# Hybrid decoder trunk on one core: the second feed-forward product taken one Strassen product at a time, its sum over the chunks kept in PSUM, and local attention's mask added by VectorE in the instruction that takes the maximum

## The chip, the cores and the metric

The kernel runs on one core of a Trainium2 chip. The core has a matrix engine (TensorE, PE in the profile, with its weight loads as PEld), three engines for elementwise work (VectorE or DVE, ScalarE or ACT, GpSimd or POOL) and a queue that issues transfers (SyncE, SP). They run side by side and wait for each other through semaphores. The metric is the device time of one execution in microseconds (us).

## The reference, cut to what matters

Two layers, 1024 tokens of width 1024, everything in float32:

```
for l in range(2):
    h = rms_norm(x, mix_norm_g[l])
    proj = h @ w_in[l]              # q, k, v of two attention branches, gates
    o_sb  = stick_breaking_attention(...)          # 8 heads
    o_swa = sliding_window_sink_attention(...)     # 8 heads, 2 key/value heads, window 128
    merged = gates[0] * (o_sb @ w_branch_sb[l]) + gates[1] * (o_swa @ w_branch_swa[l])
    x = x + merged @ w_out[l]
    h2 = rms_norm(x, mlp_norm_g[l])
    x = x + square(relu(h2 @ w_up[l])) @ w_down[l] # widths 1024 -> 4096 -> 1024
```

In local attention a block of 128 queries sees 256 keys (its own block and the one before). Scores outside the window count as minus infinity, and a learned sink per head joins the softmax: its maximum and its sum take the sink in, its output does not.

## The kernel before, in words

Every float32 product is made of three passes: each operand is split into a high part (fp32r, by ACT) and the rest (the original less the high part, by DVE), and PE computes high·high, high·low and low·high into one PSUM bank (`three`, L346 to L349).

The order of the instructions on each engine is written out ahead of time by a small planner in Python. It runs a model of the five engines and of the transfers (`Plan`): each process yields the engine that it needs and a cost, or an event or a slot to wait for, and whichever process is ready first (or has the lower rank) issues its instruction. On the chip each engine then takes its instructions strictly in that order. The costs of the model are plain numbers: `act(n)`, `dve(n)`, `mm(n)`; a transfer costs `moved(n)`, and the `LINK` table has the delay from one engine's end to the next one's start (M is the transfers, so MA is the delay from a landing to ACT).

Stages of a layer: norm of x and its transposes, gates and local attention (SWA) woven together, stick-breaking attention, merge and output projection, norm, first feed-forward product (`up_phase`), second feed-forward product (`down_phase`). There are 8 PSUM banks.

**Local attention** (`iteration` in `swa_phase`): 16 iterations in each layer, one for each of 2 key heads and 8 blocks of 128 queries, at most three in flight. Each has two PSUM banks of scores, two heads in each. Into a bank PE first writes the mask (L694: identity times a bf16 tile of zeros and -1e30, 128x512), then adds the four score matmuls (L698, 128x256 each). DVE takes the maximum of a bank (L702), two small instructions turn it into the exponent's bias (L713, L715), and ACT reads the bank with a scale and that bias, writes the exponential to `pr` in SBUF and sums it (L724).

**Second feed-forward product** (`down_phase`): u = square(relu(...)), of 1024 x 4096, is cut along its 4096 columns into four chunks c. A chunk is a 1024x1024 by 1024x1024 product, done by seven half-size products (Strassen's scheme in Winograd's form) named 1, 2, 5, 3, 6, 7, 4 in that order. The left operands (sums and differences of u's blocks) were formed in the up phase and wait in DRAM (`u_scr`). The right operands are the four quadrants 11, 12, 21, 22 of the chunk of w_down for products 1, 2 and 3, and differences of them for 5, 6, 7 and 4. A product is 4 row tiles i by 4 depth tiles j by 3 passes, 48 matmuls of 128x512. The loops run over chunks outside and products inside, `for c: for n in order`.

Before a product both its operands are split into an `operand` tile each (ACT L1273, DVE L1276, four instructions of 128x1024 on each engine for the two operands). There are five operand tiles: four of the pool "act", one of the pool "op". The differences of w_down's quadrants are made by POOL in place (`sums`, L1290, 128x512), through a tile t for product 5. At the end of every product of every chunk DVE adds the four PSUM banks to x or to an accumulator in SBUF (`collect`, L1287, L1888): 1, 5 and 6 have accumulators, which are added to the quadrants of x in the last chunk.

Between the layers the driver starts the next norm: DVE writes the normed tile `h` (L426), PE transposes it (L437), ACT and DVE split it into hT.

All transfers go through SP's queue, in the order of the plan.

Of the kernel before, what the change touches and what calls it, by code (L numbers as in the profile page):

```python
# [16 lines left out]
P = 128  # L17
# [39 lines left out]
ORDER = ("1", "2", "5", "3", "6", "7", "4")  # L57

# [48 lines left out]
class Plan:  # L107
# [6 lines left out]
    LINK = {"PA": .2, "PD": .2, "AP": .3, "DP": .26, "GP": .3, "PP": 0.0, "GD": .1, "SS": 0.0, "SM": .65, "MA": .9, "MD": .9, "MG": .9, "MP": .9, "MS": .9}  # L114
# [82 lines left out]
def tile_hybrid_trunk(ctx: ExitStack, tc: tile.TileContext, x, g_mix, g_mlp, g_rope, sinks, rope,  # L197
# [40 lines left out]
    win_mask = cp.tile([P, 256], BF16, name="win_mask")  # L238
    first_mask = cp.tile([P, 256], BF16, name="first_mask")
    nc.gpsimd.memset(win_mask, 0.0)  # L240
    nc.gpsimd.memset(first_mask, NEG)
    prev, cur = win_mask[:, 0:P], win_mask[:, P:256]
    nc.gpsimd.affine_select(out=prev, in_=prev, compare_op=ALU.is_gt, fill=NEG, base=0,
                            pattern=[[1, P]], channel_multiplier=-1)
    nc.gpsimd.affine_select(out=cur, in_=cur, compare_op=ALU.is_ge, fill=NEG, base=0,
                            pattern=[[-1, P]], channel_multiplier=1)
    nc.gpsimd.tensor_copy(first_mask[:, P:256], cur)
# [20 lines left out]
    def moved(n):  # L268

        return "M", n / 250e3, 0  # L270
# [210 lines left out]
    def swa_phase(l, base, sw, swp, hT, normed, o_scr, tab_scr, finished, tail, projected):  # L481
# [15 lines left out]
        def consts(g):  # L497
# [11 lines left out]
            if g == 0:  # L509
                yield "G", gps(512)  # L510
                nc.gpsimd.tensor_scalar(gt[:, :, 0:4], gt[:, :, 0:4], 0.125, None, ALU.mult)
# [45 lines left out]
        def iteration(g, t):  # L557
# [123 lines left out]
            msk = (first_mask if t == 0 else win_mask).unsqueeze(1).broadcast_to([P, 2, 256])  # L681
# [5 lines left out]
            zs = {}  # L687

            def scores(i):
                bz = Bank("z")  # L690
                yield from bz.take()
                yield "P", .71
                sc = bz.tile().rearrange("p (a b) -> p a b", a=2)
                nc.tensor.matmul(sc, ident_b, msk, start=True, stop=False)  # L694
                for j in range(2):
                    h = 2 * i + j
                    for kk in range(2):
                        nc.tensor.matmul(sc[:, j, lo_col:256], qst[:, h * P:(h + 1) * P], keys_[:, kk],  # L698
                                         start=False, stop=kk == 1 and j == 1)
# [3 lines left out]
                zs[i] = sc, bz  # L703
# [4 lines left out]
            yield e_y  # L708
            y5 = e_y.value
            yield e_z  # L710

            yield "D", .12
            nc.vector.scalar_tensor_tensor(mx4, mx4, -1.0, y5[:, 0:4], ALU.mult, ALU.mult)  # L713
            yield "D", .12
            nc.vector.tensor_tensor(mx4, mx4, snk[:, 1], ALU.min)  # L715
            e_s = Event(plan, 3)

            def expo(i):
                sc, bz = zs[i]
# [5 lines left out]
                bz.free()  # L725
# [947 lines left out]
    def down_phase(l, base, quads, u_scr, u_ev, tail_raw, tail_ring, wide, acc_on, x_ev, x3_ev, dst, saved, splits_done, finished):  # L1673
        r0 = base + 84000
        order = ORDER

        kinds_ = {("b", "11"): "wh", ("b", "12"): "wl", ("b", "21"): None, ("b", "22"): None}
        turns = [(c, n, j) for c in range(4) for n in order for j in range(2)]
        ring_of = (("raw", None), ("raw", None), ("wl", 0), ("wl", 1), ("wh", 2), ("wh", 3))
        spot = [Slots(plan, 1) for _ in ring_of]  # L1680
        fetched_a = {t: Event(plan) for t in turns}
        place = {(s, q, j): Slots(plan, 1) for s, q in kinds_ for j in range(2)}
        came = {(c, s, q, j): Event(plan) for c in range(4) for s, q in kinds_ for j in range(2)}
# [9 lines left out]
        def load(c, s, q, j):  # L1693
            yield place[s, q, j]
            if kinds_[s, q] is None:
                yield wide
# [27 lines left out]
        def cutting(c, n, j):  # L1724
# [11 lines left out]
            if c == 3:  # L1736
                splits_done.set()
# [433 lines left out]
```

## Time and profile before

| | us |
|---|---|
| median of 3 runs (lowest to highest) | 2814.79 (2811.83 to 2817.49) |
| the profiled execution's own time | 2815.18 |
| its span, from the first to the last instruction | 2813.4 |
| TensorE's mean granted clock, as a share of 2.4 GHz | 0.993 |

Busy time counts an instruction from start to end; matmuls overlap a little, so "busy" of PE also covers the part of an instruction that lies beside the next one. A row of instructions reads: line, engine, operation, output<-inputs, shapes, count | busy us, mean ns of one | idle time of the engine just before them, and what ended it. In a timeline a row begins with the start and the duration in us; idle time before it stands in brackets. A row of a table of stretches has: from:to in us, its length, then busy us (and instructions) of PE, PEld, DVE, ACT and POOL, the granted clock of TensorE (1.00 is 2.4 GHz, 0.50 is 1.2 GHz), the busy share of the transfer engines, and GB/s.

### The profile page before, as it was taken

What the parts mean: (1) busy time and instruction counts of PE and PEld (TensorE: products, weight loads), DVE (VectorE), ACT (ScalarE), POOL (GpSimd) and SP (SyncE); (2) the same over time, 40 slices, a digit from 0 to 9 for tenths busy, and PEclk for the clock granted to TensorE, in tenths of its full rate; (3) what the DMA queues carried; (4) which work ended last, traced back from release to release, by engine and by line L of the source; (5) the groups of instructions that cost most, each with busy time, mean ns of one, the idle gap of its engine ahead of it and who ended that gap; (6) DMA issues with size and microseconds to landing.
All of it is one profiled execution on the core that took longest, in us unless ns stands there. A gap on an engine that the chain in (4) does not pass through costs nothing.

```text
span 2813.4 us, 37269 instructions
## 1 busy us (share of the span) xinstructions
PE 2727.7 (97%) x13632; PEld 2293.8 (82%) x13632; DVE 2035.9 (72%) x3223; ACT 1269.9 (45%) x2561; POOL 493.7 (18%) x387
## 2 busy tenths in 40 slices
PE   6999999999989999999899999999999999999998
PEld 6888888888868887877678888888887788877877
DVE  5565788855587878777865657887646877777788
ACT  4776566552432223433347765655524322244332
POOL 1000000000032334323510000000000332253225
PEclk9999999999999999999999999999999999999999
DMA  4232221164034447444232222222631344564442
GB/s 164 71 91 70 60 61 58 54 228 165 31 105 161 155 143 260 151 156 144 84 116 81 80 66 59 66 56 81 220 142 31 128 146 157 157 250 154 146 151 74
DMA packets 138647, 335.50 MB, mean 119 GB/s; under 512 B 16352, under 2 KB 30688, under 8 KB 138464
## 3 DMA queue, kind: packets, MB, share of 16 engines
q1 hardware_dynamic: 138464, 333.13, 35.6%
q8 instruction: 107, 1.75, 0.3%
q14 instruction: 76, 0.62, 0.1%
HBM read 227.16 MB, written 97.52 MB: 115 GB/s over the span
## 4 chain that ended last, share of the span: by engine, by line
PE 84%; DVE 9%; ACT 4%; issue 2%; DMA 1%; POOL 1%; SPq 0%; DVEq 0%; ACTq 0%; POOLq 0%
PE bank L347 24%; PE bank L348 24%; PE bank L349 24%; DVE operand L1276 3%; PE bank L1057 2%; PE bank L1090 1%; PE bank L986 1%; PE bank L987 1%; PE bank L1089 1%; ACT pr L724 1%; PE bank L437 1%; PE bank L698 1%; DVE xt L1287 1%; PE bank L768 1%; DVE acc L1287 1%
## 5 line engine op out<-in xcount | busy, mean ns | idle before, releaser
L348 PE MATMUL bank<-operand 128*128 128x512 f32 x896 | 353.4, 394 | 27.9 <-DVE operand L1276 27.9
L347 PE MATMUL bank<-operand 128*128 128x512 f32 x896 | 351.7, 393 | 0.0
L349 PE MATMUL bank<-operand 128*128 128x512 f32 x896 | 350.8, 392 | 0.0
L1273 ACT CAST operand<-dr 128x1024 fp32r<-128x1024 f32 x208 | 205.0, 1051 | 291.4 <-PE bank L349 241.6
L1276 DVE TENSOR_TENSOR operand<-dr,operand 128x1024 fp32r<-128x1024 f32 x208 | 289.2, 1425 | 32.9 <-ACT operand L1273 32.7
L347 PE MATMUL bank<-hT,wh 128*128 128x512 f32 (+1 forms) x776 | 311.4, 401 | 1.5 <-ACT hT L394 1.5
L349 PE MATMUL bank<-hT,wl 128*128 128x512 f32 (+1 forms) x776 | 303.1, 391 | 0.0
L348 PE MATMUL bank<-hT,wh 128*128 128x512 f32 (+1 forms) x776 | 302.5, 390 | 0.1
L1273 ACT CAST wh<-raw 128x512 fp32r<-128x512 f32 x128 | 79.4, 620 | 386.2 <-DMA raw<-in_w_up_dram 201.0
L348 PEld LDWEIGHTS bank<-operand 128*128 128x128 f32 x896 | 169.5, 189 | 70.4 <-DVE operand L1276 35.9
L1290 POOL TENSOR_TENSOR stage<-raw 128x512 f32<-128x512 f32 x32 | 58.2, 1820 | 832.7 <-DMA raw<-in_w_up_dram 557.1
L347 PEld LDWEIGHTS bank<-operand 128*128 128x128 f32 x896 | 169.7, 189 | 35.6
L349 PEld LDWEIGHTS bank<-operand 128*128 128x128 f32 x896 | 169.8, 189 | 35.1
L349 PEld LDWEIGHTS bank<-hT,wl 128*128 128x128 f32 x776 | 146.8, 189 | 31.8
L347 PEld LDWEIGHTS bank<-hT,wh 128*128 128x128 f32 x776 | 147.5, 190 | 25.3 <-ACT hT L394 1.9
L348 PEld LDWEIGHTS bank<-hT,wh 128*128 128x128 f32 x776 | 147.4, 190 | 24.4 <-DVE hT L396 0.4
L336 DVE TENSOR_TENSOR wl<-raw,wh 128x1024 fp32r<-128x1024 f32 x88 | 107.5, 1222 | 71.4 <-ACT wh L333 70.8
L1287 DVE TENSOR_TENSOR xt<-xt,bank 128x512 f32<-128x512 f32 x160 | 106.3, 682 | 69.9 <-PE bank L349 69.7
L333 ACT CAST wh<-raw 128x1024 fp32r<-128x1024 f32 x88 | 92.4, 1050 | 111.5 <-PE bank L349 76.6
L1290 POOL TENSOR_TENSOR dr<-dr 128x512 f32<-128x512 f32 x64 | 115.5, 1821 | 38.3 <-issue 38.3
L1006 DVE TENSOR_TENSOR_SCAN keep<-keep 128x128 f32<-128x128 f32 (+3 forms) x128 | 99.8, 809 | 19.1 <-ACT keep L995 18.8
L1065 DVE TENSOR_TENSOR tl<-bank,th 128x512 fp32r<-128x512 f32 (+1 forms) x160 | 97.8, 629 | 20.2 <-ACT th L1063 18.9
(217 smaller groups left out, 7099.7 us busy)
## 6 DMA issues: line engine op xcount, KB each, us to landing
dr<-u_scr SPq DMA_DIRECT2D x112, 512.0 KB, 4.6
u_scr<-up SPq DMA_DIRECT2D x160, 256.0 KB, 2.6
raw<-in_w_up_dram SPq DMA_DIRECT2D x68, 512.0 KB, 4.2
dr<-in_w_down_dram SPq DMA_DIRECT2D x64, 512.0 KB, 4.3
raw<-in_w_gate_dram SPq DMA_DIRECT2D x32, 512.0 KB, 4.0
g_scr<-stage SPq DMA_DIRECT2D x64, 256.0 KB, 2.3
gate<-g_scr SPq DMA_DIRECT2D x64, 256.0 KB, 3.8
u_scr<-stage SPq DMA_DIRECT2D x64, 256.0 KB, 2.4
```

The source lines that it names most:

```text
L333: nc.scalar.copy(hi[:, :n], raw[:, :n])
L336: nc.vector.tensor_tensor(lo[:, :n], raw[:, :n], f32(hi[:, :n]), ALU.subtract)
L347: nc.tensor.matmul(ps_ap, ah, bh, start=first, stop=False)
L348: nc.tensor.matmul(ps_ap, ah, bl, start=False, stop=False)
L349: nc.tensor.matmul(ps_ap, al, bh, start=False, stop=last)
L1006: nc.vector.tensor_tensor_scan(later[:, ::-1], later[:, ::-1], later[:, ::-1], ini, ALU.mult, ALU.bypass)
L1057: nc.tensor.transpose(tr[:, i * P:(i + 1) * P], w[:, j * P - c0:(j + 1) * P - c0], ident)
L1065: nc.vector.tensor_tensor(tl[:, :n], tr[:, :n], f32(th[:, :n]), ALU.subtract)
L1273: nc.scalar.copy(op.hi(j, n), src)
L1276: nc.vector.tensor_tensor(op.lo(j, n), src, f32(op.hi(j, n)), ALU.subtract)
L1287: nc.vector.tensor_tensor(out, a, b, op)
L1290: nc.gpsimd.tensor_tensor(out, a, b, op)
```

## The change

There are three parts. The first two change what is computed where; the third changes two numbers of the planner's model, and with them the order that it writes on every engine.

1. Local attention: the mask matmuls (L694) go. The score matmuls start the bank themselves. For each head DVE runs one `tensor_tensor_reduce`: the scores (now negated, as q is scaled by -0.125) times y, with the float32 mask (+1e30) added, are written to `pr` and their minimum together with the negated sink is taken. It is built as two instructions, the pass over 128x256 and a short one that writes out the minimum. ACT then exponentiates `pr` in place. The two small instructions L713 and L715 and the reduce L702 go.
2. Second feed-forward product: the loops change places, `for n in DOWN: for c in range(4)`, with the products in the order 1, 5, 2, 6, 3, 7, 4. A product adds its four chunks in the same four PSUM banks, and DVE adds the banks to x's quadrants once, after the fourth chunk (56 additions of 128x512 in a layer; no accumulators). The quadrants of w_down are read again for each product that needs them: 88 reads of 512 KB in a layer (16 of them from `t_scr`) where there were 32, and two differences, those of products 5 and 6, are stored to `t_scr` in DRAM (16 stores) to be read back for 6 and 4. The differences are now made by DVE (128x1024), none by POOL. Six operand tiles instead of five; six places for left operands as before, and eleven for right operands.
3. The planner: the delay after a landing is 2.0 instead of 0.9, and transfers move 380e3 instead of 250e3 in its units.

```diff
+DOWN = ("1", "5", "2", "6", "3", "7", "4")
+LATE_RAWS = 3
...
-    LINK = {..., "SM": .65, "MA": .9, "MD": .9, "MG": .9, "MP": .9, "MS": .9}
+    LINK = {..., "SM": .65, "MA": 2.0, "MD": 2.0, "MG": 2.0, "MP": 2.0, "MS": 2.0}
...
-        return "M", n / 250e3, 0
+        return "M", n / 380e3, 0
...
-                yield "P", .71
+                yield "P", .48
                 sc = bz.tile().rearrange("p (a b) -> p a b", a=2)
-                nc.tensor.matmul(sc, ident_b, msk, start=True, stop=False)
                 for j in range(2):
                     h = 2 * i + j
                     for kk in range(2):
                         nc.tensor.matmul(sc[:, j, lo_col:256], qst[:, h * P:(h + 1) * P], keys_[:, kk],
-                                         start=False, stop=kk == 1 and j == 1)
+                                         start=kk == 0, stop=kk == 1)
                 z_use.done()
-                yield "D", dve(512)
-                nc.vector.tensor_reduce(mx4[:, 2 * i:2 * i + 2], sc, AX.X, ALU.max)
+                yield e_y
+                y5 = e_y.value
+                for j in range(2):
+                    h = 2 * i + j
+                    yield "D", dve(256)
+                    nc.vector.tensor_tensor_reduce(pr[:, h, lo_col:], sc[:, j, lo_col:], win_mask[:, lo_col:], y5[:, h:h + 1],
+                                                   snk[:, 1, h:h + 1], ALU.add, ALU.min, mx4[:, h:h + 1])
+                bz.free()
...
-                    nc.scalar.activation(pr[:, h], sc[:, j], AF.Exp, bias=mx4[:, h:h + 1], scale=y5[:, h:h + 1], accum_out=sm4[:, h:h + 1])
+                    nc.scalar.activation(pr[:, h, lo_col:], pr[:, h, lo_col:], AF.Exp, bias=mx4[:, h:h + 1], scale=-1.0, accum_out=sm4[:, h:h + 1])
...
+        order = DOWN
+        steps = [(n, c) for n in order for c in range(4)]
+        turns = [(n, c, j) for n, c in steps for j in range(2)]
+        a_ring = (("raw", None), ("raw", None), ("wl", 0), ("wl", 1), ("wh", 2), ("wh", 3))
+        b_ring = (("wh", 0), ("wh", 1), ("wl", 2), ("wl", 3)) + (("dr", None),) * 4 + (("late", None),) * LATE_RAWS
...
+        parts = {"1": ("11",), "2": ("21",), "5": ("12", "11"), "6": ("22", "t0"), "3": ("22",), "7": ("22", "12"), "4": ("21", "t1")}
+        keeps_ = {"5": 0, "6": 1}
...
+        opx = Slots(plan, 2)
...
+                        if m % 6 < 4:
+                            yield acts
...
+        def stream_b():
+            for n, c, j in turns:
+                for q in parts[n]:
+                    i = yield from pb.take()
+                    if q[0] == "t":
+                        yield t_in[int(q[1]), c, j]
+                        src = t_scr[int(q[1]), c, j]
+                    else:
+                        src = w_down[l, c, "12".index(q[0]) * 2 + "12".index(q[1]), j]
+                    yield "S", .45
+                    raw = pb.tile(i)
+                    nc.sync.dma_start(out=raw, in_=src)
...
+        def cut_b(n, c, j):
+            qs = parts[n]
+            yield b_in[(n, c, j), qs[0]]
+            raw, i = b_in[(n, c, j), qs[0]].value
+            use = Shared(2 if n in keeps_ else 1, lambda: pb.release(i))
+            if len(qs) > 1:
+                yield b_in[(n, c, j), qs[1]]
+                other, i2 = b_in[(n, c, j), qs[1]].value
+                yield from two("D", raw, raw, other, ALU.subtract, 1024)
+                pb.release(i2)
+                if n in keeps_:
+                    plan.spawn(keep(n, c, j, raw, use), plan.cur.rank)
+            yield ops[n, c, "b"]
+            yield from split(ops[n, c, "b"].value, 2 * j, raw, 1024)
...
+        def keep(n, c, j, raw, use):
+            yield "S", .45
+            nc.sync.dma_start(out=t_scr[keeps_[n], c, j], in_=raw)
...
+        sums = {"1": ("11", "12", "21", "22"), "2": ("11",), "5": ("12", "22"), "6": ("12", "21", "22"), "3": ("12",), "7": ("21", "22"), "4": ("21",)}
+        def product(n, c, i):
...
+                three(state[n, i][1], s.hi(j)[:, cs], s.lo(j)[:, cs], t.hi(j), t.lo(j), c == 0 and j == 0, c == 3 and j == 3)
...
+        def collect(n, i):
+            b, pm = state.pop((n, i))
+            for q in sums[n]:
+                t, h = i + 4 * (q[0] == "2"), int(q[1]) - 1
+                yield x_ev[t]
+                yield "D", dve(512)
+                xs = x_ev[t].value[:, h * 512:(h + 1) * 512]
+                nc.vector.tensor_tensor(xs, xs, pm, ALU.add)
```

**What moves on PE in local attention.** PE's order around the scores of an iteration in the first layer, before (wg is the weight of the q, k, v projection, ks and qst the split keys and queries, pr the probabilities):

```order
L349 MATMUL bank<-hT,wl 128x512
L694 LDWEIGHTS ident_b
L694 MATMUL bank<-win_mask,ident_b 128x512
L698 MATMUL bank<-ks,qst 128x256 x4
L694 LDWEIGHTS ident_b
L694 MATMUL bank<-win_mask,ident_b 128x512
L698 MATMUL bank<-ks,qst 128x256 x4
L347 MATMUL bank<-hT,wh 128x512
```

The same place in the changed kernel:

```order
L348 MATMUL bank<-hT,wl 128x512
L694 MATMUL bank<-ks,qst 128x256 x8
L346 MATMUL bank<-hT,wh 128x512
L347 MATMUL bank<-hT,wh 128x512
L348 MATMUL bank<-hT,wl 128x512
L761 MATMUL bank<-ident,pr 128x128 x4
```

The eight score matmuls of an iteration now stand together, without a mask matmul and its weight load; what fills the time until the transposes of pr is gate work (hT, wh), as before.

**What moves on SP in the second feed-forward product.** SP's queue for the loads of one whole chunk in the first layer, before (u_scr holds the left operands, in_w_down_dram the right ones):

```order
L1721 DMA dr<-u_scr_7323 128x1024 x8
L1704 DMA dr<-in_w_down_dram 128x1024
L1721 DMA dr<-u_scr_7323 128x1024 x2
L1704 DMA dr<-in_w_down_dram 128x1024 x3
L1721 DMA dr<-u_scr_7323 128x1024 x2
L1704 DMA dr<-in_w_down_dram 128x1024 x2
L1721 DMA dr<-u_scr_7323 128x1024 x2
L1704 DMA dr<-in_w_down_dram 128x1024 x2
```

SP's queue in the changed kernel, for the last loads of product 1 and the first of product 5 (t_scr takes the stored differences):

```order
L1770 DMA dr<-in_w_down_dram 128x1024 x11
L1818 DMA t_scr_7289<-dr 128x1024
L1756 DMA dr<-u_scr_7288 128x1024 x2
L1818 DMA t_scr_7289<-dr 128x1024
L1770 DMA dr<-in_w_down_dram 128x1024 x2
L1818 DMA t_scr_7289<-dr 128x1024
L1770 DMA dr<-in_w_down_dram 128x1024 x2
L1818 DMA t_scr_7289<-dr 128x1024 x2
L1770 DMA dr<-in_w_down_dram 128x1024 x2
L1756 DMA dr<-u_scr_7288 128x1024 x2
L1770 DMA dr<-in_w_down_dram 128x1024 x4
```

Before, a chunk had 14 loads of u and 8 of w_down. Now stores stand among the loads, and each of them waits for DVE's subtraction before the load behind it can be issued.

**What moves on DVE where the first layer ends.** DVE's order before the first normed tile h of the second layer, before (xt_7304 to xt_7311 are the eight row tiles of x, `v`, `rs_a` and `y` the small instructions of the norm):

```order
L1287 TENSOR_TENSOR xt_7308<-xt_7308,bank 128x512
L422 TENSOR_SCALAR v<-ss 128x1
L1287 TENSOR_TENSOR xt_7309<-xt_7309,bank 128x512 x2
L360 TENSOR_TENSOR rs_a<-y 128x1
L422 TENSOR_SCALAR v<-ss 128x1
L362 TENSOR_TENSOR rs_a<-rs_a,v 128x1
L364 TENSOR_SCALAR rs_a<-rs_a 128x1
L422 TENSOR_SCALAR v<-ss 128x1
L366 TENSOR_TENSOR y<-y,rs_a 128x1
L360 TENSOR_TENSOR rs_a<-y 128x1
L1287 TENSOR_TENSOR xt_7310<-xt_7310,bank 128x512
L426 SCALAR_TENSOR_TENSOR h<-xt_7304,y,g 128x1024
```

The same place in the changed kernel (xt_7269 is the first row tile, xt_7276 the last):

```order
L1863 TENSOR_TENSOR xt_7276<-xt_7276,bank 128x512
L1269 TENSOR_TENSOR operand<-dr,operand 128x1024 x7
L421 TENSOR_SCALAR v<-ss 128x1 x3
L359 TENSOR_TENSOR rs_a<-y 128x1
L361 TENSOR_TENSOR rs_a<-rs_a,v 128x1
L363 TENSOR_SCALAR rs_a<-rs_a 128x1
L365 TENSOR_TENSOR y<-y,rs_a 128x1
L425 SCALAR_TENSOR_TENSOR h<-xt_7269,y,g 128x1024
```

Before, the first h stood behind additions of the last product but one (7, into xt_7308 to xt_7310). Now it stands behind the last splits of operands alone; product 7's additions come earlier, since four chunks of product 4 follow it. On PE the first transposes of h stand 48 matmuls before the end of `down_phase` in the first layer before, and 90 matmuls before it now.

## Rows read from the trace of the kernel before

**Rows 1.** The page, busy time of the engines.
```profile
PE 2727.7 (97%) x13632; PEld 2293.8 (82%) x13632; DVE 2035.9 (72%) x3223; ACT 1269.9 (45%) x2561; POOL 493.7 (18%) x387
```

**Rows 2.** Waits of PE, whole span: total us, times, longest us.
```profile
PE bank L348 <- DVE operand L1276: 27.9, 17, 2.9
```

**Rows 3.** Stretches: the second feed-forward product of both layers.
```profile
1086.90:1401.20 314.30, 300.05 (x1297) 244.59 (x1295) 244.71 (x246) 116.88 (x134) 126.75 (x74) 0.99 0.43 150
2488.00:2809.70 321.70, 307.97 (x1340) 251.62 (x1339) 251.02 (x257) 113.41 (x128) 130.02 (x76) 0.99 0.44 151
```

**Rows 4.** Timeline of PE: one of six such waits.
```profile
1199.10 0.50 PE L348 MATMUL bank<-operand 128*128 128x512 f32 x1 [2.86 <-DVE operand L1276]
```

**Rows 5.** Timelines of ACT, DVE and POOL ahead of that wait.
```profile
1190.62 3.90 ACT L1273 CAST operand<-dr 128x1024 fp32r<-128x1024 f32 x4 [4.20 <-PE bank L349]
...
1191.70 6.75 DVE L1276 TENSOR_TENSOR operand<-dr,operand 128x1024 fp32r<-128x1024 f32 x3 [0.39 <-ACT operand L1273]
1198.97 1.21 DVE L1276 TENSOR_TENSOR operand<-dr,operand 128x1024 fp32r<-128x1024 f32 x1
...
1192.88 4.49 POOL L1290 TENSOR_TENSOR dr<-dr 128x512 f32<-128x512 f32 x2
```

**Rows 6.** Stretches in which TensorE's granted clock was at its lower level.
```profile
1200.30:1203.70 3.40, 3.40 (x9) 2.66 (x9) 1.22 (x1) 0.62 (x1) 3.32 (x3) 0.51 0.69 243
1405.10:1411.90 6.80, 3.91 (x14) 3.43 (x15) 6.34 (x25) 4.45 (x11) 0.00 (x0) 0.50 0.47 180
2599.80:2603.20 3.40, 3.40 (x10) 2.62 (x9) 1.22 (x1) 0.62 (x1) 3.32 (x3) 0.50 0.67 222
```

**Rows 7.** Timeline of PE: two banks of scores, from mask to mask.
```profile
189.34 0.38 PE L694 MATMUL bank<-win_mask,ident_b 128*128 128x512 bf16 x1
...
190.04 0.39 PE L694 MATMUL bank<-win_mask,ident_b 128*128 128x512 bf16 x1
```

**Rows 8.** Stretch: local attention of the first layer, past its start.
```profile
100.00:250.00 150.00, 149.41 (x864) 131.12 (x863) 93.20 (x260) 113.63 (x327) 1.89 (x3) 1.00 0.26 79
```

**Rows 9.** Groups of instructions: local attention's softmax, and their nearest kin.
```profile
L702 DVE TENSOR_REDUCE mx<-bank 128x2 f32<-128x512 f32 x64 | 42.1, 684 | 9.3 <-PE bank L698 9.3
L713 DVE SCALAR_TENSOR_TENSOR mx<-mx,y 128x4 f32<-128x4 f32 x32 | 5.0, 157 | 0.4
...
L1097 DVE TENSOR_TENSOR o<-o,bank 64x256 f32<-64x256 f32 x64 | 26.0, 406 | 16.2 <-ACT o L1095 16.0
L724 ACT ACTIVATION_READ_ACCUMULATOR pr<-bank,mx,y 128x1 f32 x128 | 25.8, 201 | 0.0
L1006 DVE TENSOR_TENSOR_SCAN keep<-keep 128x256 f32<-128x256 f32 x32 | 21.5, 673 | 0.0
```

**Rows 10.** Groups of instructions: splits and additions of the second feed-forward product.
```profile
L1276 DVE TENSOR_TENSOR operand<-dr,operand 128x1024 fp32r<-128x1024 f32 x208 | 289.2, 1425 | 32.9 <-ACT operand L1273 32.7
L1273 ACT CAST operand<-dr 128x1024 fp32r<-128x1024 f32 x208 | 205.0, 1051 | 291.4 <-PE bank L349 241.6 <-DMA dr<-u_scr 23.1 <-DVE acc L1287 17.8
L1287 DVE TENSOR_TENSOR xt<-xt,bank 128x512 f32<-128x512 f32 x160 | 106.3, 682 | 69.9 <-PE bank L349 69.7
```

**Rows 11.** Stretches in which the transfer engines were full.
```profile
1085.00:1095.00 10.00, 9.69 (x44) 7.68 (x43) 9.96 (x11) 6.19 (x8) 1.35 (x1) 1.00 1.03 413
2500.00:2510.00 10.00, 10.00 (x45) 8.25 (x45) 5.77 (x7) 2.63 (x3) 9.92 (x6) 1.00 1.06 343
```

**Rows 12.** Waits of PE from 1086 to 1130 us, then from 2486 to 2530.
```profile
PE bank L348 <- DVE operand L1276: 4.1, 5, 1.7
...
PE bank L348 <- DVE operand L1276: 3.6, 4, 1.6
```

**Rows 13.** Timelines of PE and DVE where the second layer begins.
```profile
1407.99 1.97 PE L437 MATMUL bank<-ident,h 128*128 128x128 f32 x8 [6.88 <-DVE h L426]
...
1406.65 1.28 DVE L426 SCALAR_TENSOR_TENSOR h<-xt,y,g 128x1024 f32<-128x1024 f32 x1
```

**Rows 14.** Transfers issued from 1086 to 1115 us: KB each, us to landing.
```profile
dr<-in_w_down_dram SPq DMA_DIRECT2D x5, 512.0 KB, 9.9
```

More of the change, by code (lines that the diff above doesn't have):

```diff
@@ new lines, in release, with lay @@
+            def release(self, i):
+                p = self.spots[i]
+                if i in self.final:
+                    tag, unit = self.ring[p]
+                    if unit is not None:
+                        give[unit].done()
+                    elif tag == "raw":
+                        raws.release()
+                else:
+                    self.free[p].release()
+            def lay(self, skip, first):
+                n, spots = len(self.ring), []
+                while len(spots) < self.count:
+                    spots += [p for p in range(n) if len(spots) + p >= first or p not in skip]
+                self.spots = spots[:self.count]
+                self.final = {max(i for i, p in enumerate(self.spots) if p == q) for q in set(self.spots)}
@@ L1718, in stream, with arrive, stream_a @@
+        def arrive(ev, raw, i):
+            yield moved(1024 * 512)
+            ev.set((raw, i))
+        def stream_a():
+            for n, c, j in turns:
+                i = yield from pa.take()
                 yield u_ev[c, n]
                 yield "S", .45
-                raw = wp.tile([P, 1024], F32, tag=tag, name="dr", bufs=2 if tag == "raw" else 4)
-                nc.sync.dma_start(out=raw.rearrange("p (a b) -> p a b", a=2), in_=u_scr[7 * c + order.index(n), :, 2 * j:2 * j + 2])
@@ L1739, in arrive @@
-        def arrive(ev, raw):
-            yield moved(1024 * 512)
-            ev.set(raw)
-        def loads(group):
-            for c in range(4):
-                for s, q in group:
-                    for j in range(2):
-                        yield from load(c, s, q, j)
-        def free(c, s, q, j):
-            if c < 3:
-                place[s, q, j].release()
-            elif kinds_[s, q] is not None:
-                give[j + 2 * (q == "12")].done()
-        opx = Slots(plan, 1)
@@ L1758, in operands @@
+        ops = {(n, c, s): Event(plan) for n, c in steps for s in "ab"}
+        opx = Slots(plan, 2)
         def operands():
@@ L1817, in cut_sum @@
-        def cut_sum(s, op, k, t):
-            yield from split(op, k, t, 512)
-            tmp_use[s].pop(0)()
-        tmp_use = {"a": [], "b": []}
-        def frees(c):
-            def one(s, q, j, evs):
-                for e in evs:
-                    yield e
-                free(c, s, q, j)
-                if c == 3:
-                    splits_done.set()
-            for s in "b":
-                for q in ("11", "12", "21", "22"):
-                    n = [m for m in order if m != "5" and (m, s) in source and source[m, s] == q][-1]
-                    for j in range(2):
-                        plan.spawn(one(s, q, j, [cut[c, n, s, j], summed[c, s, j]]), r0)
@@ L1853, in product @@
             yield s.ready[0]
             yield t.ready[0]
[L1855 to L1856 removed]
+            if c == 0:
+                b = Bank("md")
+                yield from b.take()
+                state[n, i] = [b, None]
+            else:
+                yield begun[n, c - 1, i]
             cs = slice(i * P, (i + 1) * P)
```

315 lines of the change are left out of this document (99 added, 216 removed).

## The prediction

> **What bounds the kernel now.** I read the page's busy times first. PE is busy for 2727.7 of 2813.4 us, the next engine for 72% [rows 1]; the reader is to see that nothing but PE's own work and its 86 idle us can give much. Then I asked who ends PE's waits: the largest line by far is DVE's split of an operand of the second feed-forward product, 27.9 us in 17 waits [rows 2]. The table of stretches puts it in place: in the two runs of that product PE is busy for 300.05 of 314.30 us and for 307.97 of 321.70 us, so 14.2 and 13.7 us are idle [rows 3]. The timelines show why. In each layer three waits are of some 2.9 us like the one at 1199.10 [rows 4]. Ahead of it ACT starts the operand's four casts only when PE gives an operand tile back at 1190.62; DVE then takes 6.75 us for three splits, while POOL takes 4.49 us for two subtractions beside them; alone a split takes 1.21 us [rows 5]. Such waits are followed by stretches at the lower level of TensorE's clock (0.50, that is 1.2 GHz): three of 3.4 us inside the two runs (the first at 1200.3, the last at 2599.8), and one of 6.8 us at 1405.1, where the second layer begins [rows 6].
>
> **Unit of work.** 1340 matmuls in 307.97 us are 0.23 us each [rows 3]. A step (one product, one chunk) is 48 of them, 11.0 us; a product's four chunks are 44 us; the 28 steps are the same in number before and after.
>
> **Part 1, the mask on PE.** From one mask matmul to the next it is 0.70 us [rows 7]. The four score matmuls between have half of 512 columns, so 4 x 0.115 = 0.46; the mask costs 0.24 (a 512-column matmul: 0.23). There are 2 layers x 16 iterations x 2 banks = 64, so 14.7 us at most. PE is busy for 149.41 of 150 us there [rows 8], so this is on the path. On DVE an iteration gives up two reduces and two small instructions, 2 x 0.684 + 2 x 0.157 = 1.68 us, and gets four passes over 128x256 with four readings of the minimum. The trace has no such pass. Bounds: half the 512-column reduce and nothing for the reading, 4 x 0.342 = 1.37 us (0.3 less than before); the 256-column scan with ACT's reading of an accumulator, 4 x (0.673 + 0.201) = 3.50 us (1.8 more) [rows 9]. I take the nearest row, an addition of 256 columns out of a bank, 0.406, with 0.157 for the reading: 4 x 0.56 = 2.25 us, 0.6 more. Over 32 iterations that is 18 us of DVE, which is busy for 93 of those 150 us [rows 8]; the cover is two other iterations in flight and the gates' matmuls. What the cover misses is a longer chain from scores to exponent, which the planner underrates (it books 0.33 for a pass). I charge a fifth, 4 us. Part 1: -14.7 + 4, about -11; from -16 (DVE faster, chain shorter) to +4 (all 18 us exposed).
>
> **Part 2, where the stalls go.** With six operand tiles and two in a step, the split of step s may begin when step s-3 ends, two steps or 22 us ahead, where the row above shows 199.10 - 190.62 = 8.5 us with five. POOL has nothing in this stage any more, so a split costs DVE its lone 1.21 us and not the mean of 1.425 [rows 5, 10]. What DVE does in a layer: 112 splits and 32 subtractions, both of 128x1024 from two SBUF tiles, at 1.21 us, and 56 additions at 0.682 us [rows 10]: 135.5 + 38.7 + 38.2 = 212 us, against 244.7 and 251.0 before [rows 3]. The tightest product is 5: 16 splits and 8 subtractions, 29 us, with the 16 additions that product 1 leaves, 10.9 us, so 40 of 44 us, behind a lead of two steps. Banks: a product holds four, the next one needs its fourth bank 3/4 of a step after its first, by which time two or three of the four old ones are added up. ACT has 112 casts of 1.051 us in 308 us and is no bound.
> What goes: 14.2 + 13.7 us of idle time, less the 4.1 and 3.6 us at the start of each run [rows 12], which I leave in, since the first operands still come through the same full transfers: 20.2 us. The three low-clock stretches inside the runs cost half of 3.4 us each, 5.1 us [rows 6]; they go too. Sum: -25.
>
> **Transfers.** Each transfer is 0.524 MB. A step of products 1, 2 and 3 needs four, of 7 and 4 six, of 5 and 6 six loads and two stores: 4.19 MB in 11.0 us, 381 GB/s, for eight of 28 steps. The trace reaches 413 GB/s with the engines full, but 343 in another full stretch with stores among the loads [rows 11]. At 413 the eight transfers take 10.2 us and nothing waits. At 343 they take 12.2 us, 1.2 us too long: 4.9 us over a product, which a cushion of two or three steps of loaded and split operands (22 us or more) takes in. I cost it at nothing; without that cover it is 16 x 1.2 = 20 us.
> The Trainium skill's page “DMA: Bandwidth & Descriptors” (section Specifications) speaks against the change: it gives about 358 GB/s as a core's share of HBM. By that figure a step of 5 or 6 would last 11.7 us, an estimate, and the sum would be 11 us worse without a cushion. Rows 11 do not bear the limit out as it stands: one stretch moved 413 GB/s.
>
> **The seam between the layers.** PE waits 6.88 us for the first normed tile, which DVE writes at 1406.65 [rows 13]; then it works for 3.9 us at half rate [rows 6], 2 us lost. Now the upper half of x is complete after product 3, two products or 88 us before the end, and the first transposes stand 90 matmuls, 20.7 us, before it. The last step's splits can begin when step (4,0) ends, 33 us before the end; four casts, four splits and two subtractions (4 x 1.21 + 2 x 1.21 = 7.3 us), a norm (about 3.5 us from x to h: ACT's square of a 1024-column tile, small instructions, 1.28 for h [rows 13]) end 22 us before it. That is just in time, so I keep 2 us: -7 (from 0 to -9).
>
> **The planner's numbers** rewrite the order everywhere, but on PE the up phase stands as before, and the head differs only in one more tile transposed ahead of the first matmuls. I cost that at nothing, give or take 2 us.
>
> **The sum.** The profiled execution took 2815.18 us (span 2813.4 and 1.8 around it), 0.4 us above the median of 2814.79. 2815.2 - 11 - 25 - 7 = 2772 us. Best case: -16, -33 (the starts go too), -9: 2757.
>
> **Rivals.**
> A. Supply: products 5 and 6 run at the rate of the slower full stretch and the cushion is not there (SP's order holds loads back): +20 us, 2792. For it: 343 GB/s with stores in the mix, and the eleven places are handed on in strict turn. Against: 413, and products 1 and 2 need only 191 GB/s, so the average from 1 to 6 is 286.
> B. The mask was free, because DVE and ACT pace local attention: part 1 gives nothing or costs 4 us: 2783 to 2787. For it: ACT is busy for 114 of those 150 us, more than any engine but PE. Against: PE's 149.41 [rows 8].
> C. The stalls aren't the split's lead but something that stays, so the change does not do what it says: only part 1 counts, 2804. Against: rows 4 and 5 give the cause piece by piece.
> D. Slower: SP's queue as the new bound. A store stands in the queue until DVE has subtracted; the loads behind it are issued after that, take up to 9.9 us to land when the engines are full [rows 14], then 1.05 + 1.21 us until PE may use them: 12 us a link. DVE in its turn waits in order for these loads, with the additions that free banks behind it. If the chain closes once a step, the lead of 22 us is eaten and each step of 5 and 6 waits. The 43 us gained are lost at 2.7 us for each of these 16 steps; at 4 us, and with a low-clock stretch of 1.7 us after each, it is 16 x 5.7 = 91 us: 2863.
>
> **How the numbers follow.** My forecast 62% (2757 to 2784 by its own bounds), A 15%, B 8%, C 6%, D 9%. A difference of 0.2% (5.6 us) is about what a measurement of this kernel can tell from none; so faster has the first four cases, 0.91, less 0.03 for a C that gives less than that; same 0.04, with 0.01 of a mild D; slower the other 0.08. The range holds the forecast, B and A and leaves out most of C and D: 2756 to 2797.
>
> **What would show each step.** Right: the line of rows 2 falls from 27.9 to some 8 us, the runs of rows 3 shrink to about 304 and 312 us with POOL at nothing, a split takes about 1.2 us on the mean, no low clock inside the runs; from 100 us on, local attention is as busy as before and 7 us shorter a layer; the new pass takes 0.35 to 0.45 us; the transposes after the first layer wait under 3 us. Wrong: transfers at a share of 1.0 all through 5 and 6 with PE waiting for splits that wait for landings (A, D), new waits of PE for DVE or ACT between 60 and 250 us (B), a wait of 2.9 us still standing in each group of steps (C).

## The result, and the profile after

The changed kernel takes 2775.2 us (median of 4 runs, 2772.4 to 2781.3) against 2813.7 us in the same comparison: a ratio of 0.9864, 95% interval 0.9842 to 0.9886, so 38.5 us faster. The forecast was 2772, and its profiled execution took 2772.42 us (span 2770.6). The profile and the experiments show, though, that three of its terms were wrong and that their errors nearly cancelled; that the sum fits so well is luck.

The page's busy times of the changed kernel, the counterpart of [rows 1]:

```profile
PE 2708.4 (98%) x13568; PEld 2281.4 (82%) x13568; DVE 1920.9 (69%) x3247; ACT 1246.6 (45%) x2521; POOL 221.1 (8%) x233
```

PE has lost the 64 mask matmuls and works 19 us less; its idle time fell from 86 to 62 us. POOL's halving, which no term of the sum counts by itself, turns out to be one half of what emptied the down phase of waits. The waits of PE in the changed kernel, whole span (total us, times, longest us), to set beside [rows 2]:

```profile
PE bank L348 <- DVE wh L1269: 6.3, 13, 0.5
PE bank L346 <- ACT operand L1266: 5.8, 4, 2.2
PE bank L347 <- DVE operand L1269: 3.0, 4, 0.8
```

The operand waits are down from 27.9 to 8.8 us, all at the start of a down run, as said. But a line with `wh`, a weight split of the *up* phase, has grown to 13 waits of half a microsecond. No term of the prediction stands for it.

To place the gains, each trace is cut at the same landmarks of PE: A, from the first transpose of local attention to the first merge matmul; U, from the first up matmul to the first down matmul; D, from the first to the last down matmul; "seam", from there to the next layer's first transpose of local attention. D1 has 32 of the 64 transposes of the next layer's h in it (8 in old_numbers), and in the kernel before also the wait of 6.88 us for the first h [rows 13]; so D1 and seam are best read as one sum. Between merge and up all traces have 180.1 us. All in us; the last column is the median of the runs.

| kernel | head | A1 | U1 | D1 | seam | A2 | U2 | D2 | median |
|---|---|---|---|---|---|---|---|---|---|
| before | 67.1 | 519.6 | 320.0 | 337.7 | 41.2 | 519.9 | 321.1 | 322.8 | 2813.7 |
| changed | 62.4 | 511.4 | 324.2 | 314.3 | 38.6 | 514.5 | 331.6 | 309.3 | 2775.2 |
| old_numbers | 65.2 | 512.4 | 321.2 | 323.8 | 47.0 | 513.1 | 320.7 | 323.6 | 2794.8 |
| numbers_alone | 62.5 | 524.4 | 324.6 | 349.6 | 40.2 | 524.5 | 328.5 | 336.3 | 2855.5 |
| numbers_split | 65.7 | 512.1 | 321.1 | 311.0 | 38.5 | 513.9 | 321.2 | 307.5 | 2757.0 |
| old_in_up | 62.8 | 514.3 | 320.4 | 311.6 | 38.3 | 514.6 | 322.1 | 307.7 | 2756.8 |
| up_late_only | 62.2 | 511.5 | 321.2 | 311.0 | 39.0 | 515.6 | 323.0 | 308.0 | 2759.0 |
| down_alone | 63.3 | 523.5 | 322.8 | 316.5 | 37.7 | 521.6 | 330.9 | 309.1 | 2791.8 |
| idle_matmul | 62.7 | 522.6 | 329.3 | 312.8 | 37.2 | 522.3 | 334.4 | 309.2 | 2795.1 |
| five_tiles | 62.3 | 511.7 | 325.9 | 314.1 | 40.6 | 514.3 | 333.0 | 309.9 | 2783.5 |
| pool_subtracts | 62.5 | 512.4 | 325.7 | 319.7 | 39.4 | 515.0 | 332.9 | 318.1 | 2791.0 |
| five_and_pool | 62.6 | 511.6 | 325.5 | 322.4 | 41.5 | 514.6 | 334.4 | 316.1 | 2794.6 |
| before_without_pool | 65.1 | 520.6 | 320.4 | 320.2 | 41.7 | 520.2 | 320.3 | 315.4 | 2788.2 |
| extra_store | 64.1 | 512.7 | 325.1 | 314.1 | 38.1 | 514.6 | 333.3 | 309.7 | 2776.0 |

Before to changed: head -4.7, attention -8.2 - 5.4, down -23.4 - 13.5, seam -2.6, and the up phase +4.2 + 10.5: -43.1 in the two traces.

Stretches of the changed kernel (us, PE, PEld, DVE, ACT, POOL busy, granted clock, DMA share, GB/s): the two down runs, and below them the two low-clock stretches, both at a start.

```profile
1077.00:1392.50 315.50, 311.00 (x1378) 256.91 (x1379) 222.80 (x254) 124.69 (x147) 0.00 (x0) 0.99 0.76 285
2455.00:2766.60 311.60, 307.35 (x1345) 253.15 (x1344) 204.12 (x207) 109.03 (x111) 0.00 (x0) 0.99 0.75 283
1079.30:1082.70 3.40, 3.29 (x8) 2.62 (x9) 2.41 (x4) 2.47 (x3) 0.00 (x0) 0.50 1.03 420
2458.30:2461.70 3.40, 3.11 (x7) 2.48 (x8) 3.40 (x5) 2.44 (x3) 0.00 (x0) 0.50 1.03 410
```

Against [rows 3], POOL is at nothing, DVE has fallen to 204 to 223 us (212 were predicted) and the transfers have nearly doubled. Behind the start of the runs PE has no wait of note and never falls to the lower clock. The two stretches at the starts are new: the kernel before had three inside its runs and none at a start. Groups of instructions, beside [rows 9, 10]:

```profile
L1269 DVE TENSOR_TENSOR operand<-dr,operand 128x1024 fp32r<-128x1024 f32 x224 | 262.7, 1218 | 121.0 <-ACT operand L1266 117.9 <-DMA dr<-in_w_down_dram 3.1
L703 DVE CUSTOM_DVE_ANT_0 pr<-bank,win_mask,snk 128x256 f32<-128x256 f32 x112 | 55.7, 538 | 16.0 <-PE bank L694 16.0
```

A split takes its lone 1.22 us everywhere. The new pass takes 0.538 us, outside the 0.35 to 0.45 given as its sign and 0.13 more than the 0.406 taken for it; the reading of its minimum takes 0.081 where 0.157 was taken. Together that is 0.62 us a head, close to the 0.56 charged.

### The profile page after: what moved, and what is told of

The parts are those of the page before. It is cut to its first block, busy times and chain, and to the rows that moved or that the text cites. A ratio compares the mean times of both kernels' runs of the same rounds, so it can differ in the third digit from the quotient of the medians.

```text
span 2770.6 us, 37073 instructions
## 1 busy us (share of the span) xinstructions
PE 2708.4 (98%) x13568; PEld 2281.4 (82%) x13568; DVE 1920.9 (69%) x3247; ACT 1246.6 (45%) x2521; POOL 221.1 (8%) x233
## 5 line engine op out<-in xcount | busy, mean ns | idle before, releaser
L1266 ACT CAST operand<-dr 128x1024 fp32r<-128x1024 f32 x224 | 220.1, 1049 | 369.7 <-PE bank L348 173.7
L1269 DVE TENSOR_TENSOR operand<-dr,operand 128x1024 fp32r<-128x1024 f32 x224 | 262.7, 1218 | 121.0 <-ACT operand L1266 117.9
L1269 DVE TENSOR_TENSOR wh<-raw,wh 128x512 fp32r<-128x512 f32 x128 | 102.5, 801 | 146.7 <-ACT wh L1266 146.7
L988 ACT ACTIVATE keep<-bank 128x128 f32<-128x128 f32 (+1 forms) x192 | 91.3, 499 | 38.9 <-PE bank L982 23.4
```

The costliest lines, as they stand in the source:

```text
L988: nc.scalar.activation(keep[:, lo:512], z, AF.Sigmoid, scale=-1.0)
L1266: nc.scalar.copy(op.hi(j, n), src)
L1269: nc.vector.tensor_tensor(op.lo(j, n), src, f32(op.hi(j, n)), ALU.subtract)
```

## The experiments

**The planner's numbers.** Five kernels ask where the up phase's 14.7 us come from.

old_numbers is the changed kernel with

```
-    "MA": 2.0, ... "MS": 2.0          return "M", n / 380e3, 0
+    "MA": .9, ... "MS": .9            return "M", n / 250e3, 0
```

> The changed kernel with the planner's old numbers (0.9 us after a transfer, 250e3 elements per us). The trace of the changed kernel shows its up phases 4.2 and 10.5 us longer than before (324.1 and 331.6 us against 320.0 and 321.1, from the first up matmul to the first down matmul). Theory N, the planner's numbers moved the splits of the up phase: both are back at 320 to 321 us, and the time is 2775 - 15 = 2760 us if the down phase does not need the new numbers. Rival R, the new down phase itself disturbs the end of the up phase (its first loads, its tiles): up phases stay at 324 and 332, 2775 within 3 us. Third, the numbers belong to the down phase: up phases at 320 and 321, but the down runs longer than their 315.5 and 311.6 us, with a time between 2760 and 2775 or above.

2794.8 us (ratio to before 0.993, 0.9918 to 0.9943). The third case: the up phases are back at 321, but the down runs grow by 9.5 and 14.3 us and the seam by 8.4. Timeline of ACT, then of PE, then of DVE, in old_numbers where product 1 ends:

```profile
1111.84 3.90 ACT L1266 CAST operand<-dr 128x1024 fp32r<-128x1024 f32 x4 [8.87 <-PE bank L348]
1130.01 1.04 ACT L1266 CAST operand<-dr 128x1024 fp32r<-128x1024 f32 x1 [14.26 <-DVE dr L1280]
...
1131.10 0.80 PE L346 MATMUL bank<-operand 128*128 128x512 f32 x1 [8.42 <-ACT operand L1266]
...
1120.43 5.46 DVE L1863 TENSOR_TENSOR xt<-xt,bank 128x512 f32<-128x512 f32 x9
1125.81 1.22 DVE L1269 TENSOR_TENSOR operand<-dr,operand 128x1024 fp32r<-128x1024 f32 x1
1126.94 0.68 DVE L1863 TENSOR_TENSOR xt<-xt,bank 128x512 f32<-128x512 f32 x1
1127.54 1.22 DVE L1269 TENSOR_TENSOR operand<-dr,operand 128x1024 fp32r<-128x1024 f32 x1
1128.68 1.22 DVE L1280 TENSOR_TENSOR dr<-dr 128x1024 f32<-128x1024 f32 x1
```

With the old numbers DVE's first subtraction for product 5 (1128.68) stands behind product 1's additions and four splits, the last two of which are shown; ACT's cast waits for it and PE for the cast, 8.42 us. The granted clock is at 0.50 for 10.2 us from 1125.6 on, 4.7 us of them after the wait. DVE in the changed kernel at the same place of the second layer:

```profile
2499.74 5.46 DVE L1863 TENSOR_TENSOR xt<-xt,bank 128x512 f32<-128x512 f32 x9
2505.12 1.21 DVE L1280 TENSOR_TENSOR dr<-dr 128x1024 f32<-128x1024 f32 x1
2506.25 2.47 DVE L1863 TENSOR_TENSOR xt<-xt,bank 128x512 f32<-128x512 f32 x4
2508.64 1.22 DVE L1269 TENSOR_TENSOR operand<-dr,operand 128x1024 fp32r<-128x1024 f32 x1
```

Here it stands ahead of the splits and of the last additions, and PE does not wait. So the same instructions in another order are worth 32 us in the down phase and the seam.

numbers_alone is the kernel before with the same two lines changed the other way.

> The kernel before with only the planner's two numbers changed. Theory N: the up phases grow to some 324 and 332 us, and the time is 2814 + 15 = 2829 us, give or take 5 for what the order does to the old down phase. Rival R (the loss belongs to the new down phase): up phases at 320 and 321, 2814 within 3 us.

2855.5 us (1.0144, 1.013 to 1.0158), 26 us more than theory N's 2829. The up phases grow to 324.6 and 328.5, the way it says; but the old down phase loses another 25.4 us and the old attention 9.4. The numbers suit the new down phase and neither the old one nor the up phase.

numbers_split is the changed kernel with the two lines of old_numbers and, in the down phase's transfers (load and store), the new numbers written out:

```
-            yield moved(1024 * 512)
+            yield "M", 1024 * 512 / 380e3, 0
+            yield 2.0
```

> The changed kernel with the old numbers everywhere but in the down phase, whose loads and stores keep the new ones (380e3 per us, 2.0 us after a transfer). Theory N: up phases at 320 to 321 us with the down runs as in the changed kernel, 2760 us, faster than both kernels. Rival R: 2775 within 3 us, up phases at 324 and 332.

2757.0 us (0.9795, 0.9782 to 0.9809): 18 us faster than the changed kernel. Up at 321, down at 311.0 and 307.5. Which of the two numbers does it? The next two kernels change the up phase's two transfers alone, the first to both old numbers, the second to the old rate with the new 2.0 us:

```
-            yield moved(1024 * 512)               # the load; the store's 512 * 512 likewise
+            yield "M", 1024 * 512 / 250e3, 0
+            yield .9                              # 2.0 in up_late_only
```

> The changed kernel with the old numbers (250e3 elements per us, 0.9 us) in the up phase's loads and stores alone. Theory N: up phases back from 324.1 and 331.6 to 321 us, the head's gain of 3 us kept: 2775 - 14 = 2761, as low as 2754 if the head's gain adds to the run with the numbers split (2757). If the loss comes from what the other phases plan: 2770 or above.

> As the run before this one, but with the new 2.0 us after a transfer and only the old rate (250e3) in the up phase. If the later arrival that the planner assumes is what puts the splits behind other work of DVE: up phases of 324 us and more and 2770 or above. If it is the rate (transfers planned closer together): up phases at 321 and 2757 to 2761.

2756.8 (0.9795, 0.9781 to 0.9808) and 2759.0 (0.9801, 0.9788 to 0.9814). With the old rate the loss is gone whichever delay stands beside it, so the loss needs the new rate: transfers planned closer together. Whether the new rate with the old 0.9 us would lose as much was not run. Waits of ACT and DVE in the second up phase, changed kernel:

```profile
ACT wh L1266 <- POOL raw L1283: 129.3, 28, 9.6
...
DVE wh L1269 <- ACT wh L1266: 79.0, 15, 6.7
```

In up_late_only the two are 8.4 and 1.9 us, in the kernel before 83.4 and 7.2; in old_in_up they are

```profile
ACT wh L1266 <- POOL raw L1283: 81.2, 16, 8.5
...
DVE wh L1269 <- ACT wh L1266: 13.2, 11, 3.9
```

So the wait that comes and goes with the loss is DVE's: it stands in its queue before a split whose cast waits for POOL's subtraction, and what is queued behind reaches PE late. PE's idle time is 6.6 of the 10.5 us that the second up phase loses. Which instruction moved first was not traced further.

**The mask.**

down_alone puts the old local attention back into the changed kernel (mask matmul, reduce, two small DVE instructions, exponent from the bank).

> The changed kernel with the local attention of before (mask added by PE, maximum by a reduce of DVE). By the landmarks of the two traces part 1 was worth 8.2 + 5.4 = 13.6 us, so 2775 + 13.6 = 2789 us. By the prediction's charge of 4 us for a longer chain: 2786. Rival B (the mask was free, since DVE and ACT pace that stage): 2775 within 3 us.

2791.8 us (0.9918, 0.9904 to 0.9931), 16.6 more than the changed kernel. idle_matmul keeps DVE's new pass and gives PE a matmul that nothing reads:

```
+                nc.tensor.matmul(zt.rearrange("p (a b) -> p a b", a=4), ident_b, sb_mask.unsqueeze(1).broadcast_to([P, 4, P]), start=True, stop=True)
```

> The changed kernel with one more matmul of 512 columns at the place of the old mask matmul, whose result nothing reads; DVE still adds the mask. It gives back PE's 64 x 0.23 = 14.7 us and leaves DVE's chain as changed. If PE alone paced local attention: 2775 + 15 = 2790. If the longer chain on DVE had cost the 4 us that the prediction charges, the added PE time would hide it: 2775 + 11 = 2786. If DVE and ACT pace the stage (rival B): 2775 within 3 us.

2795.1 us (0.9931, 0.9914 to 0.9947). The two A stretches sum to 1044.9 us here, 1045.1 in down_alone and 1025.9 in the changed kernel: with PE's matmul put back it no longer matters which of the two softmax chains DVE has. So part 1 is PE's time. From before to changed PE's busy time in the two A stretches falls by 15.9 us and its idle time rises from 1.3 to 3.6: 2.4 us at the most for DVE's longer chain, where 4 were charged. Under the new numbers the mask is dearer than 0.23 us: 19.0 us for 64 is 0.30. With the old numbers the same change is worth 14.0 (1039.5 to 1025.5, before to old_numbers), 0.22 each. Why the mask costs 5 us more under the new numbers was not tried; idle_matmul's time also has up phases that are 7.9 us longer than the changed kernel's.

**The stalls of the down phase.**

five_tiles:

```
-                    if m % 6 < 4:   ... opx = Slots(plan, 2)   bufs=2
+                    if m % 5 < 4:   ... opx = Slots(plan, 1)   bufs=1
```

> The changed kernel with five operand tiles in the down phase, as before, in place of six; POOL stays idle there. Theory L (the prediction's: the stalls went because two whole steps of operands can be split ahead): the waits of some 2.9 us come back in each group of steps, 20 us with their low clock, so 2775 + 20 = 2795 us. Rival Q (the stalls went because DVE's splits take 1.22 us instead of 2.25 beside POOL, and DVE has less to do): four casts and three splits at 1.21 us fit behind the release of a tile, no waits inside the runs, 2775 within 4 us.

D is 314.1 and 309.9 us, as in the changed kernel, and no wait stands inside the runs. The median, 2783.5 (0.9891, 0.9868 to 0.9913), is 8 us above with overlapping intervals, so neither forecast of the time is met; in the trace the difference stands in the up phases (3.1 us) and the seam (2.0). The lead of two steps, the reason that the prediction gave, is not what took the stalls away.

pool_subtracts gives the subtractions to POOL, with six tiles:

```
-                yield from two("D", raw, raw, other, ALU.subtract, 1024)
+                yield from two("G", raw, raw, other, ALU.subtract, 1024)
```

> The changed kernel with the 32 subtractions a layer of the down phase on POOL in place of DVE; six operand tiles. POOL took 2.25 us for 128x512 beside the splits before, so some 4.5 us for 128x1024, 9 us in a step of 11 us. Theory L (lead): six tiles hide it, the splits beside it take up to 2.25 us but the run stays within 5 us: 2775 to 2780. Rival Q (DVE beside POOL is what stalled): splits of 1.4 us and more on the mean, waits of PE for DVE's operand splits in products 5, 6, 7 and 4, and 20 us or more: 2795 or above.

2791.0 us (0.9923, 0.9905 to 0.9942). DVE and POOL ahead of the one long wait of the second layer, then PE:

```profile
2508.61 4.58 DVE L1269 TENSOR_TENSOR operand<-dr,operand 128x1024 fp32r<-128x1024 f32 x2 [8.52 <-ACT operand L1266]
2513.11 0.68 DVE L1863 TENSOR_TENSOR xt<-xt,bank 128x512 f32<-128x512 f32 x1
2513.71 2.82 DVE L1269 TENSOR_TENSOR operand<-dr,operand 128x1024 fp32r<-128x1024 f32 x1
2516.45 5.46 DVE L1863 TENSOR_TENSOR xt<-xt,bank 128x512 f32<-128x512 f32 x9
2521.83 1.21 DVE L1269 TENSOR_TENSOR operand<-dr,operand 128x1024 fp32r<-128x1024 f32 x1
...
2506.20 12.59 POOL L1283 TENSOR_TENSOR dr<-dr 128x1024 f32<-128x1024 f32 x4 [0.23 <-DMA dr<-in_w_down_dram]
...
2523.10 0.80 PE L347 MATMUL bank<-operand 128*128 128x512 f32 x1 [3.14 <-DVE operand L1269]
```

Beside POOL a split takes 2.3 to 2.8 us instead of 1.22; an addition out of a bank keeps its 0.68. DVE has no gap in these rows, so the three stretched splits put the one at 2521.83, which PE waits for, 3.7 us later; the wait is 3.14. The time lies between the two forecasts: D grows by 14.2 us, and the long waits behind the start are one in each layer, where product 5 begins, not one in every group. five_and_pool has both edits:

> The changed kernel with both: five operand tiles and the down phase's 32 subtractions a layer on POOL. Alone, five tiles left the down runs at 314.1 and 309.9 us (changed kernel: 314.4 and 309.3) and POOL's subtractions made them 319.7 and 318.1. Theory C (each cover is enough alone; the stalls of before needed both, few tiles and late partners from POOL): runs of 325 us and more, waits of some 3 us in most steps of products 5, 6, 7 and 4, and 2805 us or above. Rival Q (POOL's lateness alone counts, tiles do not): as with POOL alone, 319 us a run and 2791 within 5.

2794.6 us (0.9931, 0.9918 to 0.9945), D 322.4 and 316.1: as with POOL alone within the runs' spread. Theory C falls. That says more than the run was made for: with POOL at work and five tiles, as before, the new loops still have no wait in each chunk, and the second layer's D is 6.7 us below that of the kernel before.

before_without_pool is the kernel before with one letter changed, five tiles and all its partial sums kept (the planner writes the order anew):

```
-SUM = {"a": "D", "b": "G"}
+SUM = {"a": "D", "b": "D"}
```

> The kernel before, five operand tiles, with the subtractions of its second operand on DVE in place of POOL (80 of 128x512 a layer, 0.68 us each, 54 us more on DVE; its splits lose their stretched cases of 2.3 us). Theory Q: the three waits of 2.9 us a layer disappear, and down runs shrink from 337.7 by some 8 us or more, unless DVE's 54 us make new waits elsewhere. Theory L (five tiles are the cause): the waits of 2.9 us stay, and with DVE's added work the runs are 338 us or longer.

2788.2 us (0.9906, 0.9893 to 0.992): 26.7 us less than before, from one letter. D shrinks by 17.5 and 7.4 us although DVE takes over 64 subtractions a layer (not the 80 of the expectation), 44 us; its busy time in D grows by only 8 to 10 us, since its splits take 1.235 us on the mean and not 1.425. The three waits of 2.9 us are gone, and the wait for the first h falls from 6.88 to 0.79 us. The one long wait left behind the start in each layer, 3.56 us, stands beside the only work that POOL still has, 12 last additions. PE, DVE and POOL there:

```profile
2760.90 0.80 PE L348 MATMUL bank<-operand 128*128 128x512 f32 x1 [3.56 <-DVE operand L1276]
...
2754.10 1.40 DVE L1287 TENSOR_TENSOR xt<-xt,acc 128x512 f32<-128x512 f32 x1
2755.43 1.78 DVE L1287 TENSOR_TENSOR acc<-acc,stage 128x512 f32<-128x512 f32 x1
2757.13 0.68 DVE L1287 TENSOR_TENSOR acc<-acc,bank 128x512 f32<-128x512 f32 x1
2757.73 1.37 DVE L1287 TENSOR_TENSOR xt<-xt,acc 128x512 f32<-128x512 f32 x1
...
2753.66 3.00 POOL L1290 TENSOR_TENSOR xt<-xt,acc 128x512 f32<-128x512 f32 x2 [11.58 <-DVE acc L1287]
2757.29 1.27 POOL L1290 TENSOR_TENSOR xt<-xt,acc 128x512 f32<-128x512 f32 x1 [0.62 <-DVE acc L1287]
```

**The transfers.** extra_store makes each store of a subtracted tile twice.

```
+            nc.sync.dma_start(out=t_scr[2 + keeps_[n], c, j], in_=raw)
```

> The changed kernel with each store of a subtracted tile made twice (to another place that nothing reads): 16 more stores of 0.524 MB a layer, so a step of products 5 and 6 moves 5.24 MB in 11.0 us, 476 GB/s, more than any stretch of the traces has shown (413). If the transfers have a cushion of two steps (the prediction's): 12.7 us a step at 413 GB/s, 1.7 us too long, 13.6 us over the eight steps of a layer, of which the cushion takes all but a few us: 2775 to 2783. Rival A (no cushion): 2 x 8 x 1.7 = 27 us, 2802, more if the rate is nearer 343.

2776.0 us (0.9866, 0.9848 to 0.9884), no loss. Three stretches of a step's length there, from the middle of product 5 on:

```profile
1148.00:1159.00 11.00, 11.00 (x50) 9.12 (x49) 10.61 (x10) 6.07 (x7) 0.00 (x0) 1.00 1.03 417
1159.00:1170.00 11.00, 11.00 (x51) 9.09 (x49) 6.12 (x8) 4.22 (x5) 0.00 (x0) 1.00 1.03 413
1170.00:1181.00 11.00, 11.00 (x50) 9.13 (x49) 9.30 (x11) 3.91 (x4) 0.00 (x0) 1.00 1.02 414
```

The engines are full for 33 us at 413 to 417 GB/s, and PE is busy for all of it: the cushion is there, and rival A had none of its price.

## Why the prediction came out right, and which steps were wrong

- **The sum.** -11 - 25 - 7 = -43 was forecast, -43.1 stands between the traces. Measured: attention -13.6, down runs and seam -39.5 (forecast: 32), head -4.7 (nothing), up phase +14.7 (nothing). Gains that were larger than forecast made up for a loss that was left out: the fit of the sum is luck.
- **Part 1 (-11).** The 14.7 us of PE were right; of the 4 us charged for the chain at most 2.4 show. Rival B is refuted by down_alone and idle_matmul.
- **Part 2 (-25).** The place, the waits and DVE's 212 us were right; the second run is 309.3 us where about 312 was said (the rows for the first run end 48 matmuls before its end). The low clock was right in part: three stretches inside the runs went, two at the starts came. The step that failed is the cause: "With six operand tiles and two in a step, the split of step s may begin when step s-3 ends". Five tiles leave the runs as they are. The split that PE waited for in [rows 4] is not one of the three of [rows 5] but the next one on DVE, a piece of product 5's right operand out of the tile t; all six waits of 2.9 us of the kernel before end with such a piece:

```profile
1198.37 0.68 DVE L1276 TENSOR_TENSOR operand<-t,operand 128x512 fp32r<-128x512 f32 x1
```

  Ahead of it three splits took 6.75 us beside POOL, 3.1 us more than alone, and the wait was 2.86 us. "POOL has nothing in this stage any more", the other half of the same paragraph, says what ends that.
- **POOL is not the whole cause.** In the second layer's D, which holds no seam, POOL's subtractions taken out of the old loops give 7.4 us (before_without_pool), the new loops and order with POOL at work and five tiles give 6.7 (five_and_pool), both together 13.5. In D1 with the seam it is 17.0, 15.0 and 26.0. Each alone ends the three waits of 2.9 us a layer. What in the new loops does it stays open: they have no tile t, and DVE has fewer additions in them, but neither was tried alone. Rival C, that the stalls stay, did not happen.
- **What before_without_pool lacks** of the changed kernel's D is 5.9 and 6.1 us; its wait of 3.56 us beside POOL's last additions and 6.8 us at half clock, 3.56 + 3.4 = 7.0 us a layer, would cover that. That nothing else is in it is argued from these rows, not tried.
- **Transfers and SP's queue (nothing).** Right: rivals A and D did not happen, even with two more stores a step. (The 9.9 us of [rows 14] that D is built on are a median, not the most.)
- **The seam (-7).** The wait of 6.88 us for the first h is gone, and the first transposes stand at 1368.3, 24 us before the end of D1. But product order is not the only way: with the old order of products and POOL's subtractions on DVE it is 0.79 us (before_without_pool), and with the new one and the old numbers PE still waits 4.17 us among these transposes (old_numbers). So product order alone does not give it, and it can be had without.
- **The planner's numbers (nothing, give or take 2).** Wrong, the largest miss: "on PE the up phase stands as before" is true and tells nothing, because the queues that moved are those of DVE, ACT and SP. They cost 14.7 us in the up phase; without them the changed kernel is 19.6 us slower, since the down phase needs them. The loss in the up phase needs the new rate (up_late_only).

The Trainium skill's page “SBUF — State Buffer” (section Who interferes with whom) says that a DVE instruction with two inputs in SBUF contends with a GpSimd instruction that reads SBUF, and that one with at most one SBUF input does not, outside the 2-port perf modes. The traces agree: 2.29 against 1.22 us for a split of two tiles, 1.4 to 1.78 against 0.68 for an addition of two tiles, and 0.68 unchanged where one operand is in a bank. By that rule a good half of the gain in the down phase could have been read as the end of POOL's work.

## What to carry to other kernels

Before crediting a deeper buffer with the end of a stall, look up which instruction the wait ended with, and compare the late engine's durations ahead of it with its lone durations: if the excess covers the wait, try first to move the neighbour's work; here one letter in the old kernel gave 27 us, where the whole change gave 38. Where a planner orders the queues, a change of its constants is a change of every phase: compare each engine's queue, not PE's alone, and let phases with different transfer loads keep constants of their own, which gave another 18 us here.

## What the runs showed of the hardware

- 413 to 417 GB/s with stores among the loads, for 33 us on end; the 343 GB/s of [rows 11] was not a bound of the mix.
- DVE's pass that adds the mask out of a bank and takes a minimum costs 0.538 us for 128x256, 0.13 more than an addition of 256 columns, and 0.081 for the reading, less than half of ACT's 0.201 [rows 9].
- POOL's subtraction of 128x1024 took 2.74 us on the mean (pool_subtracts), where 4.5 were expected from twice its 128x512 beside DVE's splits.
- DVE beside POOL: a split of two SBUF tiles of 128x1024 took 2.29 to 2.82 us instead of 1.22, an addition with one operand in a bank kept its 0.68 (pool_subtracts).
